# Fourier input and gate of each 256-token tile by seven block products instead of eight, with the gate transposed on TensorE and kept in DRAM

## The chip, the cores and the metric

The kernel runs on one core of one Trainium2 chip. The metric is the device time of one execution in microseconds (us). The engines are called PE (TensorE; PEld is its weight load), DVE (VectorE), ACT (ScalarE), POOL (GpSimd) and SP (SyncE, which issues most DMAs).

## The reference

One layer of a hybrid token mixer on 2048 latent tokens of width 1024, with 256 context tokens as a prefix. All in float32:

```python
h = modulate(rms_norm(x, g_pre[layer]), shift, scale)
f_in, f_gate, q, k, v, r_gate = jnp.split(h @ w_in[layer], IN_SPLITS, axis=-1)
...
u = f_in.reshape(bsz, length, N_FOURIER_GROUPS, FOURIER_GROUP)
mixed = jnp.real(jnp.fft.fft2(u, axes=(1, 3), norm='ortho'))
y = jnp.einsum('blgc,gcd->blgd', mixed, w_fourier)
return y * jax.nn.silu(f_gate)
...
y = jnp.concatenate([fourier, retention], axis=-1) @ w_out[layer]
x_next = x + gate * rms_norm(y, g_post[layer])
```

w_in has 3072 columns: six blocks of 512, in the order f, gate, q, k, v, r_gate. The change concerns `h @ w_in` for the first two, f and its gate, which are 2048 x 1024 by 1024 x 1024.

## The kernel before, in words

TensorE multiplies in a 32-bit form of lower precision, so every float32 operand is split into a high part (a copy on ACT) and a low part (the difference, on DVE or POOL), and every product is three matmuls: high by high, high by low, low by high. A projection (`proj`, L176 to L181) of 128 tokens by 512 columns is thus 8 blocks of the inner dimension by 3, 24 matmuls of 128x512.

The stages in the order of time. First the adaLN vectors and the context. Then a loop over tiles t = 1 to 7 of 256 tokens: the normed and modulated tile h is kept in DRAM, and k, v and r_gate of its two chunks are projected, with the tails of the retention states (`kv_tail1`, `kv_tail2`) between them. Then the f stage, a loop over eight tiles again, each made of the two chunks of 128 tokens that the first step of the Fourier transform pairs (`FB`): `hf_split` splits h as read back, `fin` projects f (pf, 2 times 24 matmuls of 128x512), `butterfly` makes the steps of the transform over tokens on DVE in the blocks R, and `fgate` makes the gate (pfg) with the weights as the stationary operand, 4 times 24 matmuls of 128x256. That leaves the gate transposed, channels on partitions, as the later stage needs it; ACT writes Silu of it into four tiles sg in SBUF. `gate_acc` and `gate_fin` (the adaLN gate of the output, two matmuls pg) are spread over the same loop.

Then follows a block whose order is written by hand for all engines (L1251 on). Four residue classes of the transform come one after the other, in the order 2, 1, 5, 0, each in four groups g: `ops_pair` makes its operands from R (two scaled copies ta and tb on ACT, sums on DVE, then for each of four sums bt a cast on ACT and a low part op, on DVE for the first and on POOL for the second of a pair); T (`cls_T`, pT) multiplies them by a table; Th and Tl are T's high and low part, made by ACT and DVE; Y (`cls_y`, pp and pq) multiplies by the folded Fourier weights (weo); POOL multiplies the result into sg (`gate`, L945). Generators in the list bg hold work for DVE, ACT and POOL, and `pull(n)` lets n steps of it run between two T's. In the block before, T and Y of the first two classes run beside the splits of the q weights (wq); then q of the last pair of chunks (`q_steps(7)`, four products of 24 matmuls of 128x256, each two followed by the rotation on DVE and POOL); then class 5 beside the first retention chunk; then class 0, the other chunks and the output projection.

PE's order in the f stage is left to the scheduler before and is written by hand after; DVE, ACT, POOL and SP are left to it there in both.

Of the kernel before, what the change touches and what calls it, by code (L numbers as in the profile page):

```python
# [10 lines left out]
F32 = mybir.dt.float32  # L11
# [19 lines left out]
def hymba_kernel(ctx: ExitStack, tc: tile.TileContext, a: dict, out: bass.AP):  # L31
# [12 lines left out]
    def unit(shape, dt, name):  # L44
        return units.tile(shape, dt, tag="unit", name=name)
# [7 lines left out]
    def lo_of(dst, src, hi):  # L53
        nc.vector.tensor_tensor(out=dst, in0=src, in1=hi.bitcast(F32), op=ALU.subtract)  # L54
# [471 lines left out]
    hraw = {}  # L526

    def h_load(t):
        hraw[t] = []
        for b in range(2):  # L530
            hr = w4.tile([P, KT, P], F32, tag="w4", name=f"hr{t}")
            nc.sync.dma_start(out=hr, in_=d_h[FB[t][b] // 2][:, :, FB[t][b] % 2 * P:(FB[t][b] % 2 + 1) * P])
            hraw[t].append(hr)

    def hf_split(t):
        hi, lo = unit([P, KT, 256], F32R, f"fhi{t}"), unit([P, KT, 256], F32R, f"flo{t}")
        for b, hr in enumerate(hraw.pop(t)):
            bs = slice(b * P, (b + 1) * P)
            nc.scalar.copy(hi[:, :, bs], hr)
            lo_of(lo[:, :, bs], hr, hi[:, :, bs])  # L540
        hls[t] = (hi, lo)
# [185 lines left out]
    for t in range(1, NT):  # L727
        hi, lo = hls.pop(t)
        for b in range(2):
            c = 2 * t + b  # L730
            tok = slice(b * P, (b + 1) * P)
            p1 = ps("pk")
            proj(p1, hi, lo, tok, wk_u)
            kr = kr_of(p1, c)
            kv_tail1(*pend[0])
            p2 = ps("pv")
            proj(p2, hi, lo, tok, wv_u)
            v = v_of(p2, c)
            kv_tail2(*pend[0])
            pend[:] = [(c, kr, v, *kv_operands(kr, v))]  # L740
            if b == 0 and t + 1 < NT:
                x_prep(t + 1)
            if b == 1 and t + 2 < NT:
                x_tile(t + 2)
            if t == 3 and b == 0:
                decay_tables()
            if t == NT - 1 and b == 0:
                wf_u, bg = load_w("wf", a["w_in"], 0)
                h_load(0)
            if t == NT - 1 and b == 1:  # L750
                hf_split(0)
                h_load(1)
            for f in bg[:3]:
                f()
            bg = bg[3:]
            p3 = ps("pr")
            proj(p3, hi, lo, tok, wr_u)
            rg_of(p3, c)


    wg_u, bg = load_w("wg", a["w_in"], 512)
    sg = [unit([P, SEQ], F32, f"sg{g}") for g in range(4)]
    R = [unit([P, 4, 512], F32, f"R{i}") for i in range(4)]

    def blk(j):
        return R[j // 4][:, j % 4, :]

    def fgate_g(t, g):
        hi, lo = hls[t]
        pg = ps("pfg", (P, 256))  # L770
        for kt in range(KT):
            whi = wg_u[kt // 2][:, 0, kt % 2, g * P:(g + 1) * P]
            wlo = wg_u[kt // 2][:, 1, kt % 2, g * P:(g + 1) * P]
            mm(pg, whi, hi[:, kt, :], start=(kt == 0), stop=False)  # L774
            mm(pg, whi, lo[:, kt, :], start=False, stop=False)  # L775
            mm(pg, wlo, hi[:, kt, :], start=False, stop=(kt == KT - 1))  # L776
        dst = sg[g].rearrange("p (b c n) -> p b c n", b=2, n=P)[:, :, FB[t][0], :]
        nc.scalar.activation(dst, pg.rearrange("p (b n) -> p b n", b=2), AF.Silu)
        if g == 3:
            hls.pop(t)  # L780

    def fgate(t):
        for g in range(4):
            fgate_g(t, g)

# [24 lines left out]

    def two(dst, x, y, sign):

        nc.vector.scalar_tensor_tensor(out=dst, in0=x, scalar=2.0, in1=y, op0=ALU.mult,
                                       op1=ALU.add if sign > 0 else ALU.subtract)
# [5 lines left out]
    def fin(t, b):  # L820
        hi, lo = hls[t]
        pf = ps("pf")
        proj(pf, hi, lo, slice(b * P, (b + 1) * P), wf_u)
        j = FB[t][0]
        if b == 0:
            nc.scalar.copy(blk(j), pf)
        else:
            tt(blk(j + 8), blk(j), pf, ALU.subtract)
            tt(blk(j), blk(j), pf, ALU.add)
# [136 lines left out]

    wfs = load_wf()
    h_load(2)
    for t in range(NT):
        if t + 1 < NT:  # L970
            hf_split(t + 1)
        if 0 < t and t + 2 < NT:
            h_load(t + 2)
        fin(t, 0)
        if t == 0:
            kv_tail1(*pend[0])
            for f in bg[:3]:
                f()
        fin(t, 1)
        if t == 0:  # L980
            kv_tail2(*pend[0])
            for f in bg[3:]:
                f()
        butterfly(t)
        if t < NT - 2:
            fgate(t)
        if 1 <= t <= 4:
            gate_acc(2 * (t - 1))
            gate_acc(2 * (t - 1) + 1)
        if t == 5:  # L990
            gate_fin()


# [39 lines left out]
    def q_steps(p):  # L1033
# [7 lines left out]
        def q(s):  # L1041
            if s % 2 == 0:
                pq.append(ps("pq"))
            o = pq[s // 2][:, s % 2 * 256:s % 2 * 256 + 256]
            for kt in range(KT):
                h = hq[p, kt // 4]
                whi = wq_u[kt // 2][:, 0, kt % 2, s * P:(s + 1) * P]
                wlo = wq_u[kt // 2][:, 1, kt % 2, s * P:(s + 1) * P]
                mm(o, whi, h[:, 0, kt % 4], start=(kt == 0), stop=False)  # L1049
                mm(o, wlo, h[:, 0, kt % 4], start=False, stop=False)  # L1050
                mm(o, whi, h[:, 1, kt % 4], start=False, stop=(kt == KT - 1))  # L1051
            if s % 2:
                rot_q(s // 2)
# [196 lines left out]

    with tc.manual_schedule(engines={ENG.PE, ENG.DVE, ENG.Activation, ENG.Pool, ENG.SP}):  # L1251
        load_tab(0)
        raw_q = w_load(a["w_in"], 1024)
        fgate_g(NT - 2, 0)
        bg.append(gen1(ops_pair(2)))
        pull(9)
        fgate_g(NT - 2, 1)
        fold_wf(*wfs)
        for g in range(2, 4):
            fgate_g(NT - 2, g)  # L1260
        load_tab(1)
        bg.append(gen1(ops_pair(1)))
        pull(2)
        fgate_g(NT - 1, 0)
        pull(2)
        fgate_g(NT - 1, 1)
        pull(2)
        fgate_g(NT - 1, 2)
        fgate_g(NT - 1, 3)
        pull(9)  # L1270
        wq_u = w_units("wq")
        load_h(7, 0)
        load_h(7, 1)
# [6 lines left out]
        for kt in range(KT):  # L1280
            bg.append(gen(lambda kt=kt: w_split(wq_u, kt, raw_q[kt // 2][:, kt % 2, :],
                                                eng=gp_ if kt % 2 and kt < 7 else nc.vector)))
            if kt == 3:
                bg.append(gen(lambda: split_h(7, 0)))
        bg.append(gen(lambda: split_h(7, 1)))
        pend = []
        for k in range(2):
            for g in range(4):
# [3 lines left out]
                pull(1)  # L1292
# [8 lines left out]
        for f in q_steps(7):  # L1301
            f()
# [234 lines left out]
```

## Time and profile before

| quantity | value |
|---|---|
| median of 3 runs | 925.33 us (925.31 to 925.96) |
| the profiled execution | 924.87 us |
| its span, first to last instruction | 923.0 us |
| PE matmuls, share of the span | 97%, 5412 of them |
| DVE / ACT / POOL, share of the span | 56% / 35% / 30% |
| mean granted clock of TensorE | 0.990 |

A row of the timeline gives the start, the duration, the engine and line, the output and inputs by the program's names, and in brackets how long the engine had been idle and what ended that. The duration of one matmul is longer than the distance of two starts, as matmuls are pipelined. The page cuts the span in 40 slices with the busy share of each in tenths. A row of windows gives the busy time of each engine in a stretch, with the number of instructions, and at its end the granted clock, the share of the DMA engines and GB/s. A row of groups ends with busy time, mean ns and the idle time just ahead.

### The profile page before, as it was taken

To read this page: it belongs to the slowest core of one execution; us is meant where nothing else is said; L and a number is where in the kernel's file an instruction comes from. 1 tells how busy PE (TensorE), PEld (TensorE's weight loads), DVE (VectorE), ACT (ScalarE), POOL (GpSimd) and SP (SyncE) were. 2 spreads that over 40 slices of the span, in tenths; PEclk is the share of its full clock that TensorE was granted. 3 is DMA by queue.
4 is the path that set the end of the run, shared out by engine and by line. 5 is a ranking of instruction groups with operands and counts; after the bars stand their busy time and mean duration, and the time that the engine had idled before them with its cause. 6 is when DMAs were issued, how large, how long until landed. Compare 5 with 4: busy or idle time off the path is not lost.

```text
span 923.0 us, 14211 instructions
## 1 busy us (share of the span) xinstructions
PE 898.6 (97%) x5412; PEld 788.5 (85%) x5412; DVE 517.8 (56%) x1020; ACT 325.6 (35%) x654; POOL 275.2 (30%) x342
## 2 busy tenths in 40 slices
PE   7899999999999999999999998999999999999997
PEld 6678888888888888999998898998888989989885
DVE  3455655254353842332512569998677767777552
ACT  3444862262222432211111153543243334333331
POOL 2106331222122111000000056765343434443352
PEclk8999999999999999999999999899999999999999
DMA  8935683363442843633311146579545554344412
GB/s 298 395 132 222 210 312 120 122 241 121 164 168 88 291 130 130 205 95 96 96 61 47 47 138 211 189 246 343 193 144 184 184 180 172 106 145 129 145 58 92
DMA packets 76309, 153.47 MB, mean 166 GB/s; under 512 B 6096, under 2 KB 32976, under 8 KB 70480
## 3 DMA queue, kind: packets, MB, share of 16 engines
q1 hardware_dynamic: 74976, 146.26, 45.9%
q0 software_dynamic: 1120, 6.29, 2.0%
q8 instruction: 43, 0.70, 0.3%
q14 instruction: 26, 0.21, 0.1%
q10 hardware_dynamic: 144, 0.00, 0.0%
HBM read 107.71 MB, written 44.83 MB: 165 GB/s over the span
## 4 chain that ended last, share of the span: by engine, by line
PE 84%; DVE 6%; DMA 4%; ACT 2%; issue 2%; POOL 1%; SPq 0%; DVEq 0%; POOLq 0%; ACTq 0%
PE pout L180 5%; PE pout L181 5%; PE pout L179 5%; PE pfg L776 3%; PE pfg L775 3%; PE pfg L774 3%; PE pr L179 3%; PE pr L180 3%; PE pf L179 3%; PE pf L180 3%; PE pr L181 3%; PE pf L181 3%; PE pv L179 3%; PE pv L181 3%; PE pk L181 3%; PE pv L180 3%
## 5 line engine op out<-in xcount | busy, mean ns | idle before, releaser
L179 PE MATMUL pout<-wo,y 128*128 128x512 f32 x256 | 102.0, 399 | 0.0
L180 PE MATMUL pout<-wo,y 128*128 128x512 f32 x256 | 99.8, 390 | 1.7 <-DVE wo L151 1.7
L181 PE MATMUL pout<-wo,y 128*128 128x512 f32 x256 | 100.1, 391 | 0.4 <-DVE y L54 0.4
L1051 PE MATMUL pq<-hq,wq 128*128 128x256 f32 x256 | 72.5, 283 | 0.6 <-DVE hq L54 0.6
L1049 PE MATMUL pq<-hq,wq 128*128 128x256 f32 x256 | 73.0, 285 | 0.0
L774 PE MATMUL pfg<-fhi,wg 128*128 128x256 f32 x256 | 72.7, 284 | 0.0
L1050 PE MATMUL pq<-hq,wq 128*128 128x256 f32 x256 | 72.5, 283 | 0.0
L775 PE MATMUL pfg<-flo,wg 128*128 128x256 f32 x256 | 72.3, 283 | 0.0
L776 PE MATMUL pfg<-fhi,wg 128*128 128x256 f32 x256 | 72.0, 283 | 0.0
L205 POOL TENSOR_TENSOR ka<-ka,kb 128x512 f32<-128x512 f32 x16 | 20.9, 1309 | 129.0 <-DVE kb L57 98.4
L241 POOL TENSOR_TENSOR vd<-v,dk 128x256 f32<-128x256 f32 x64 | 43.8, 715 | 51.8 <-ACT v L563 30.1
L226 DVE SCALAR_TENSOR_TENSOR Sf<-Sf,dk,pkv 128x128 f32<-128x128 f32 x64 | 19.3, 345 | 69.9 <-PE pkv L256 68.3
L180 PEld LDWEIGHTS pout<-wo,y 128*128 128x128 f32 x256 | 48.2, 188 | 11.4 <-DVE wo L151 2.1
L181 PEld LDWEIGHTS pout<-wo,y 128*128 128x128 f32 x256 | 48.0, 188 | 11.2 <-DVE y L54 0.9
L179 PEld LDWEIGHTS pout<-wo,y 128*128 128x128 f32 x256 | 48.2, 188 | 9.0
L1206 POOL TENSOR_TENSOR xo<-xo,t 128x512 f32<-128x512 f32 x30 | 44.4, 1500 | 22.8 <-DMA xo<-in_x 12.6
L179 PE MATMUL pf<-wf,fhi 128*128 128x512 f32 x128 | 50.4, 393 | 0.0
L856 POOL DMA_DIRECT2D tab<-in_tabs x4 | 2.6, 648 | 159.4 <-PE pf L181 159.4
L180 PE MATMUL pf<-wf,fhi 128*128 128x512 f32 x128 | 49.9, 389 | 0.0
L181 PE MATMUL pf<-wf,flo 128*128 128x512 f32 x128 | 49.8, 389 | 0.0
L1051 PEld LDWEIGHTS pq<-hq,wq 128*128 128x128 f32 x256 | 49.1, 192 | 0.8 <-DVE hq L54 0.8
L774 PEld LDWEIGHTS pfg<-fhi,wg 128*128 128x128 f32 x256 | 49.1, 192 | 0.5 <-issue 0.2
(293 smaller groups left out, 2550.4 us busy)
## 6 DMA issues: line engine op xcount, KB each, us to landing
sd<-d_st SPq DMA_DIRECT2D x16, 1024.0 KB, 5.5
wraw<-in_w_in SPq DMA_DIRECT2D x20, 512.0 KB, 5.1
ada<-in_ada_ss SPq DMA_DIRECT2D x8, 1024.0 KB, 12.9
hr<-d_h SPq DMA_DIRECT2D x16, 512.0 KB, 5.0
out<-xo SPq DMA_DIRECT2D x32, 256.0 KB, 2.1
xo<-in_x SPq DMA_DIRECT2D x30, 256.0 KB, 3.5
xtx<-in_xT SPq DMA_DIRECT2D x7, 1024.0 KB, 7.0
xk<-in_x SPq DMA_DIRECT2D x14, 512.0 KB, 6.1
```

The source lines that it names most:

```text
L179: mm(o, hi[:, kt, tok], whi, start=first, stop=False)
L180: mm(o, hi[:, kt, tok], wlo, start=False, stop=False)
L181: mm(o, lo[:, kt, tok], whi, start=False, stop=last)
L205: nc.gpsimd.tensor_tensor(out=ra, in0=ra, in1=rb.rearrange("p h a f -> p h (a f)"), op=ALU.add)
L241: nc.gpsimd.tensor_tensor(out=t[:, :, i, :], in0=v[:, hs, :], in1=d[:, hs].unsqueeze(2).to_broadcast([P, 2, P]), op=ALU.mult)
L774: mm(pg, whi, hi[:, kt, :], start=(kt == 0), stop=False)
L775: mm(pg, whi, lo[:, kt, :], start=False, stop=False)
L776: mm(pg, wlo, hi[:, kt, :], start=False, stop=(kt == KT - 1))
L1049: mm(o, whi, h[:, 0, kt % 4], start=(kt == 0), stop=False)
L1050: mm(o, wlo, h[:, 0, kt % 4], start=False, stop=False)
L1051: mm(o, whi, h[:, 1, kt % 4], start=False, stop=(kt == KT - 1))
L1206: nc.gpsimd.tensor_tensor(out=xo, in0=xo, in1=ch.t[j], op=ALU.add)
```

## The change

For one tile, h is a 2 x 2 matrix of blocks: two chunks of 128 tokens by two halves of the inner dimension (A11 to A22). The weights are 2 x 2 blocks of 512 x 512: two halves of the inner dimension by f and gate (B11 to B22). The four result blocks (f and gate of the two chunks) took eight block products; after the change they take seven, by Strassen's scheme in Winograd's form. The sums of weight blocks, T1 to T4, are made once by DVE beside tile 7 of the x loop, where they and B11, B21, B22 are split; the sums of h, S1 to S4, are made for each tile by `h_comb`, which runs for tile t + 1 while tile t is multiplied. A block product (`product`) is 12 matmuls of 128x512. The products of a tile accumulate in three PSUM banks, X, Y and Z; between two products into one bank its sum so far is copied by ACT (p1, u2, p5) or added up by DVE (fg, R).

The gate of a chunk now comes out with tokens on partitions. `fg_T` turns it by four TensorE transposes into PSUM during the next tile, ACT writes Silu of it to a work tile, and SP stores it to DRAM (d_sg); ahead of the T and Y stage it is loaded back as four tiles sg of 1 MB. `gate_acc` and `gate_fin` move into the x loop. The wq weights are split during the last tile, and q of pair 7 moves ahead of T(0,0), its rotation split in two steps (rots); `ops_pair(1)` comes after it, and two steps of the list are pulled after each T of the first class. The diff, cut to its core:

```diff
-    def fgate_g(t, g):
-        hi, lo = hls[t]
-        pg = ps("pfg", (P, 256))
-        for kt in range(KT):
-            whi = wg_u[kt // 2][:, 0, kt % 2, g * P:(g + 1) * P]
-            wlo = wg_u[kt // 2][:, 1, kt % 2, g * P:(g + 1) * P]
-            mm(pg, whi, hi[:, kt, :], start=(kt == 0), stop=False)
-            mm(pg, whi, lo[:, kt, :], start=False, stop=False)
-            mm(pg, wlo, hi[:, kt, :], start=False, stop=(kt == KT - 1))
...
+    def h_comb(t):
+
+        a11, a12, a21, a22 = hraw.pop(t)
...
+        hl_split(A["A11"], a11)
+        hl_split(A["A12"], a12)
+        tt(s1, a21, a22, ALU.add)
+        tt(s2, s1, a11, ALU.subtract)
+        hl_split(A["S2"], s2)
+        hl_split(A["S1"], s1)
+        hl_split(A["A22"], a22)
+        tt(a21, a11, a21, ALU.subtract)
+        hl_split(A["S3"], a21)
+        tt(a12, a12, s2, ALU.subtract)
+        hl_split(A["S4"], a12)
...
+    def b_T1():
+        for i in range(2):
+            x, y = b_load(0, 1, i), b_load(0, 0, i)
+            tt(x, x, y, ALU.subtract)
+            b_split("T1", i, x)
...
+    def b_T4():
+        for i in range(2):
+            x = b_load(1, 0, i)
+            less(x, "T2", i)
+            b_split("T4", i, x)
...
+    b_plain("B22", 1, 1)
+    h_comb(0)
+    h_raw(1)
+    b_T4()
+    rg_part(NCH - 1, hi, lo, toks[1])
...
+    def product(o, A, B, first):
+
+        for kt in range(4):
+            whi, wlo = B[kt // 2][:, 0, kt % 2, :], B[kt // 2][:, 1, kt % 2, :]
+            for i, (x, w) in enumerate(((0, whi), (0, wlo), (1, whi))):
+                mm(o, A[:, x, kt, :], w, start=(first and kt + i == 0),
+                   stop=(kt + i == 5), skip_group_check=not first)
...
+    def fg_T(t, b):
+
+        x, c = fgs.pop((t, b)), FB[t][b]
+        pt = ps("pfT")
+        for g in range(4):
+            nc.tensor.transpose(pt[:, g * P:(g + 1) * P], x[:, g * P:(g + 1) * P], ident)
+        s_ = wk([P, 4, P], "sgt")
+        nc.scalar.activation(s_, pt.rearrange("p (g n) -> p g n", g=4), AF.Silu)
+        nc.sync.dma_start(out=d_sg[:, :, c * P:(c + 1) * P].rearrange("g p n -> p g n"), in_=s_)
...
+        X = ps("pX")
+        product(X, A["A11"], Bw["B11"], True)
+        p1 = copy_of(X, "p1")
+        if t:
+            fg_T(t - 1, 1)
...
+        Y = ps("pY")
+        product(Y, A["A12"], Bw["B21"], True)
+        tt(blk(j), Y, p1, ALU.add)
+        if t:
+            fg_T(t - 1, 0)
...
+        product(X, A["S2"], Bw["T2"], False)
+        u2 = copy_of(X, "u2")
+        Z = ps("pZ")
...
+        h_comb(t + 1)
+        product(Z, A["S1"], Bw["T1"], True)
+        p5 = copy_of(Z, "p5")
+        product(X, A["S3"], Bw["T3"], False)
+        fg_sum(t, 1, X, p5)
+        product(Z, A["S4"], Bw["B22"], False)
+        fg_sum(t, 0, Z, u2)
+        product(X, A["A22"], Bw["T4"], False)
+        f_second(j, X)
+        butterfly(t)
+        if t + 2 < NT:
+            h_raw(t + 2)
...
-    for t in range(NT):
-        if t + 1 < NT:
-            hf_split(t + 1)
-        if 0 < t and t + 2 < NT:
-            h_load(t + 2)
-        fin(t, 0)
...
-        fin(t, 1)
...
-        butterfly(t)
-        if t < NT - 2:
-            fgate(t)
...
     with tc.manual_schedule(engines={ENG.PE, ENG.DVE, ENG.Activation, ENG.Pool, ENG.SP}):
...
+        X, Z, A = last["X"], last["Z"], last["A"]
+        product(Z, A["S1"], Bw["T1"], True)
+        p5 = copy_of(Z, "p5")
+        product(Z, A["S4"], Bw["B22"], False)
+        fg_sum(NT - 1, 1, X, p5)
+        fg_sum(NT - 1, 0, Z, last["u2"])
         bg.append(gen1(ops_pair(2)))
         pull(9)
-        fgate_g(NT - 2, 1)
+        rots = []
+        q7 = q_steps(7, rots)
+        q7[0]()
+        q7[1]()
+        fg_T(NT - 1, 1)
+        fg_T(NT - 1, 0)
+        sg = [unit([P, SEQ], F32, f"sg{g}") for g in range(4)]
+        for g in range(4):
+            nc.sync.dma_start(out=sg[g], in_=d_sg[g])
+        q7[2]()
         fold_wf(*wfs)
...
+        q7[3]()
+        rots[0]()
         load_tab(1)
         bg.append(gen1(ops_pair(1)))
...
-            bg.append(gen(lambda kt=kt: w_split(wq_u, kt, raw_q[kt // 2][:, kt % 2, :],
-                                                eng=gp_ if kt % 2 and kt < 7 else nc.vector)))
...
                 if len(pend) > 2:
                     Y(*pend.pop(0))
-                pull(1)
+                pull(2 - k)
+                if (k, g) == (0, 0):
+                    rots[1]()
                 if (k, g) == (0, 3):
                     bg.append(gen1(ops_pair(5)))
                     load_tab(2)
...
-        for f in q_steps(7):
-            f()
         bg.append(gen1(ops_even()))
```

How PE's instructions stand at the end of the f stage. Before, the last rows ahead of T(0,0) are the gate of tile 7 (pfg), and T's rows (pT) follow at once:

```order
L774 MATMUL pfg<-fhi_4396,wg_3269 128x256
L775 MATMUL pfg<-flo_4397,wg_3269 128x256
L776 MATMUL pfg<-fhi_4396,wg_3269 128x256
L917 MATMUL pT<-tab_4521,op_4557 128x2x128
L918 MATMUL pT<-tab_4521,op_4557 128x2x128
L919 MATMUL pT<-tab_4521,op_4557 128x2x128
```

After, these are the last two products of tile 7 (pX is the product with T3, pZ the ones with T1 and B22) and the first matmuls of q (pq):

```order
L892 MATMUL pZ<-T_3016,S_4390 128x512 x4
L892 MATMUL pX<-T_3133,S_4391 128x512 x6
L892 MATMUL pX<-T_3134,S_4391 128x512 x6
L892 MATMUL pZ<-T_3016,S_4390 128x512 x2
L892 MATMUL pZ<-B_3310,S_4391 128x512 x6
L892 MATMUL pZ<-B_3311,S_4391 128x512 x6
L1164 MATMUL pq<-hq_4562,wq_4542 128x256
L1165 MATMUL pq<-hq_4562,wq_4542 128x256
L1166 MATMUL pq<-hq_4562,wq_4542 128x256
```

Only two matmuls of the product with T1 are left between the product with T3 and the one with B22, which reuses Z; and q, which came after the Y's of the second class, now stands ahead of the T's.

How DVE's instructions stand from the first low part of T (Tl) on. Before, the operands of class 1 (op, from bt) are done by then, and the wq splits stand between the Tl and the y:

```order
L57 TENSOR_TENSOR bt<-R_3277,tb 128x512
L57 TENSOR_TENSOR bt<-R_3276,ta 128x512
L851 TENSOR_TENSOR op_4671<-bt,op_4671 128x512
L57 TENSOR_TENSOR bt<-R_3277,tb 128x512
L54 TENSOR_TENSOR Tl<-pT,Th 128x512
L149 TENSOR_TENSOR wq_4798<-wraw,wq_4798 128x512
L54 TENSOR_TENSOR Tl<-pT,Th 128x512 x2
L57 TENSOR_TENSOR y_4871<-p_sb,pq 128x256 x2
L149 TENSOR_TENSOR wq_4799<-wraw,wq_4799 128x512
L54 TENSOR_TENSOR Tl<-pT,Th 128x512
L57 TENSOR_TENSOR y_4905<-p_sb,pq 128x256 x2
```

After, the operands of class 1 and the second rotation of q (qa, qb, qt) stand there:

```order
L54 TENSOR_TENSOR Tl<-pT,Th 128x512
L901 SCALAR_TENSOR_TENSOR ta<-R_3395,ta 128x512
L901 SCALAR_TENSOR_TENSOR tb<-R_3396,tb 128x512
L57 TENSOR_TENSOR qa<-pq,qcs 128x512
L57 TENSOR_TENSOR qb<-pq,qcs 128x512
L1183 TENSOR_TENSOR qt<-qb,qa 64x256
L1183 TENSOR_TENSOR qt<-qa,qb 64x256
L54 TENSOR_TENSOR Tl<-pT,Th 128x512
L57 TENSOR_TENSOR bt<-R_3395,ta 128x512
L993 TENSOR_TENSOR op_4830<-bt,op_4830 128x512
L57 TENSOR_TENSOR bt<-R_3396,tb 128x512
L54 TENSOR_TENSOR Tl<-pT,Th 128x512
```

What moved is `ops_pair(1)`, from ahead of T(0,0) to between the T's, and the rotation, which came after the Y's; the wq splits went the other way.

How DVE's instructions stand in tile 0 of the f stage, which is new. The rows ahead of the sum fg that frees bank X (the last split of tile 0's own sums stands further up):

```order
L57 TENSOR_TENSOR braw<-braw,T_3130 128x1024
...
L57 TENSOR_TENSOR braw<-braw,T_3130 128x1024
L54 TENSOR_TENSOR A_3480<-hr_3345,A_3480 128x512
L57 TENSOR_TENSOR hs_3478<-hs_3477,hr_3343 128x512
L57 TENSOR_TENSOR hr_3347<-hr_3343,hr_3347 128x512
L54 TENSOR_TENSOR T_3355<-braw,T_3355 128x1024
L57 TENSOR_TENSOR R_3393<-pY,p_3414 128x512
L54 TENSOR_TENSOR T_3356<-braw,T_3356 128x1024
L57 TENSOR_TENSOR hr_3345<-hr_3345,hs_3478 128x512
L57 TENSOR_TENSOR fg<-pX,p_3514 128x512
```

braw are raw weight blocks on the way to T4 (T_3355, T_3356), and hr, hs and A_3479 belong to tile 1: all of this stands ahead of fg.

251 lines of the change are left out of this document (148 added, 103 removed).

## The prediction

> **What bounds the kernel now.** I read the page's first part, the slices, the chain and the groups; then the timeline of TensorE; then the windows of the stages that change. The page says that the matmul stream is nearly the span, and that the chain runs through it.
>
> ```profile
> PE 898.6 (97%) x5412; PEld 788.5 (85%) x5412; DVE 517.8 (56%) x1020; ACT 325.6 (35%) x654; POOL 275.2 (30%) x342
> PE   7899999999999999999999998999999999999997
> DVE  3455655254353842332512569998677767777552
> PE 84%; DVE 6%; DMA 4%; ACT 2%; issue 2%; POOL 1%; SPq 0%; DVEq 0%; POOLq 0%; ACTq 0%
> ```
>
> A slice is 23 us. In slices 16 to 22, counted from 0 (369 to 531 us, f and gate products), TensorE reads 9 and DVE 1 to 5 tenths: a matmul less there is time less. In slices 24 to 26 (554 to 623) DVE reads 9: the next stage is not TensorE's. The windows show it (columns: time, then busy time and count of PE, PEld, DVE, ACT and POOL, then the clock, DMA share and GB/s):
>
> ```profile
> 357.87:518.00 160.13, 160.13 (x984) 144.01 (x983) 50.73 (x65) 31.20 (x56) 0.81 (x1) 1.00 0.32 96
> 542.50:561.20 18.70, 17.70 (x146) 17.29 (x145) 14.20 (x24) 11.58 (x27) 14.58 (x16) 1.00 0.51 169
> 561.20:572.85 11.65, 11.65 (x99) 11.65 (x98) 10.96 (x12) 2.50 (x5) 7.94 (x9) 1.00 0.65 229
> 572.85:578.00 5.15, 2.72 (x15) 1.90 (x14) 4.40 (x7) 1.32 (x3) 3.04 (x3) 0.85 0.92 304
> 578.00:583.00 5.00, 5.00 (x25) 5.00 (x25) 4.87 (x8) 3.24 (x6) 3.98 (x5) 0.50 0.13 50
> 640.00:923.00 283.00, 275.61 (x1668) 245.54 (x1666) 184.92 (x443) 92.20 (x214) 112.39 (x124) 1.00 0.43 149
> ```
>
> The rows are f and gates; the T and Y of two classes; q of pair 7, 11.65 us of pure matmuls under which the operands of class 5 are made (DVE 10.96); the head of T(2,0), which waits; a stretch at half clock; and the rest. After 640 the TensorE is full again, so a lead gained earlier is kept to the end.
>
> **Term 1: matmuls.** Durations of single matmuls overlap, so I take the pitch of starts, and the counts from the groups (three rows a product; the first and last are shown).
>
> ```profile
> 339.82 0.39 PE L180 MATMUL pk<-wk,hhix 128*128 128x512 f32 x1
> ...
> 344.81 0.39 PE L181 MATMUL pk<-wk,hlox 128*128 128x512 f32 x1
> 345.05 0.60 PE L506 MATMUL pkT<-ident,ka 128*128 128x128 f32 x4
> ...
> 345.71 0.40 PE L180 MATMUL pv<-wv,hhix 128*128 128x512 f32 x1
> ...
> 419.80 0.28 PE L774 MATMUL pfg<-fhi,wg 128*128 128x256 f32 x1
> ...
> 426.88 0.28 PE L776 MATMUL pfg<-fhi,wg 128*128 128x256 f32 x1
> ```
>
> The groups of the page (count, then busy time and mean):
>
> ```profile
> L774 PE MATMUL pfg<-fhi,wg 128*128 128x256 f32 x256 | 72.7, 284 | 0.0
> L776 PE MATMUL pfg<-fhi,wg 128*128 128x256 f32 x256 | 72.0, 283 | 0.0
> L179 PE MATMUL pf<-wf,fhi 128*128 128x512 f32 x128 | 50.4, 393 | 0.0
> L181 PE MATMUL pf<-wf,flo 128*128 128x512 f32 x128 | 49.8, 389 | 0.0
> ```
>
> Wide: (344.81 − 339.82)/22 = 0.2268 us. Half wide: (426.88 − 419.80)/59 = 0.120. Removed: 384 × 0.2268 + 768 × 0.120 = 87.1 + 92.2 = 179.3. Added: 8 tiles × 7 products × 12 = 672 wide ones, 152.4, not 7/8 of 179.3, since a wide matmul is cheaper per column. Four transposes and the step behind them take 345.71 − 345.05 = 0.66, less one matmul 0.44; the gate needs 16 such groups, 7.1. Net 179.3 − 159.5 = **−19.8 us**. The Trainium skill, "TensorE: Matmul & The Clock Gate", Part 4, gives about 275 ns for a transpose in a kernel's context; by that 64 would take 17.6 us, as an estimate, and the term would be −9.3; the trace has 0.11 us each in a row of four and decides. The q of pair 7 and the two adaLN matmuls only move: zero, as both lie on TensorE before and after.
>
> **Term 2: new waits inside f.** A product reuses the bank that a copy or a sum must have read, and DVE now makes the operands of the next tile. The prices:
>
> ```profile
> 495.93 1.22 DVE L54 TENSOR_TENSOR flo<-hr,fhi 128x1024 fp32r<-128x1024 f32 x1
> 519.35 1.29 DVE L57 TENSOR_TENSOR R<-R,R 128x512 f32<-128x512 f32 x2
> ...
> 501.20 0.39 PE L181 MATMUL pf<-wf,flo 128*128 128x512 f32 x1
> 501.63 0.59 ACT L826 COPY R<-pf 128x512 f32<-128x512 f32 x1 [5.01 <-PE pf L181]
> ```
>
> A tile is 84 × 0.2268 + 2 × 0.44 = 19.9 us of TensorE. DVE has 7 lo parts, 4 combinations, 5 sums and about 3 butterfly passes, 19 of 128x512 at 0.61 to 0.68: 11.6 to 13; ACT 12 passes of 0.59, 7.1. Both fit, so middle tiles cost nothing, unless the order on DVE makes a sum late (rival 2). Two places have no room. Tile 0: the last product into X (A22·T4) waits for the sum fg, and that stands behind both halves of T4 and tile 1's first combinations: 4 subtractions at 1.15, 2 lo parts at 1.22 and 8 small passes at 0.605, 11.9 us from where the tile's own splits end. That is, by my walk, 8.3 us into the tile; fg is done at 20.2, the product could start at 18.3 (6 products, transposes and kv products at 0.12): +1.9, between 0 (splits end by 6.4) and 4. Last tile: between Z's end and the next product into Z only two matmuls stand, and the copy p5 needs 0.43 + 0.59 after the last start: 1.02, less the pitch, about +0.9, between 0.6 and 1.5. Sum **+2.8**. The splits of the B blocks (14 lo parts and 12 subtractions, 30 us at 1.15) lie beside tile 7's projections, where DVE is at 2 to 4 tenths (slices 14 and 15): zero, up to 2 if they run late into tile 0.
>
> **Term 3: the cover that q gave.** With q of pair 7 ahead, nothing of TensorE's is left between the Y's and T(2,0); the operands of classes 1 and 5 are made between the T's. Before, T(0,0) starts at 542.50 and T(2,0)'s head ends near 578.1, 35.6 us, of which q is 11.65: net 23.95. Its waits today:
>
> ```profile
> 574.36 0.38 PE L919 MATMUL pT<-tab,op 128*128 128x256 f32 x1 [0.75 <-POOL op L851]
> ...
> 577.55 0.58 PE L919 MATMUL pT<-tab,op 128*128 128x256 f32 x1 [0.82 <-POOL op L851]
> ```
>
> The same timeline for DVE and POOL, where one DVE pass coincides with a run of gates:
>
> ```profile
> 565.71 4.01 DVE L817 SCALAR_TENSOR_TENSOR tb<-R,tb 128x512 f32<-128x512 f32 x1
> ...
> 565.79 3.37 POOL L945 TENSOR_TENSOR sg<-y,sg 128x256 f32<-128x256 f32 x4
> ```
>
> And the groups by shape:
>
> ```profile
> L849 ACT CAST op<-bt 128x512 fp32r<-128x512 f32 x12 | 7.4, 620 | 23.2 <-DVE bt L57 23.2
> L851 POOL TENSOR_TENSOR op<-bt,op 128x512 fp32r<-128x512 f32 x6 | 7.7, 1288 | 29.1 <-ACT op L849 23.3 <-PE pq L1051 3.9 <-issue 1.9
> L57 DVE TENSOR_TENSOR y<-p_sb,pq 128x256 f32<-128x256 f32 x24 | 8.8, 407 | 0.0
> L1065 DVE TENSOR_TENSOR qt<-qa,qb 64x256 f32<-64x256 f32 x16 | 14.3, 891 | 0.4
> L1065 DVE TENSOR_TENSOR qt<-qb,qa 64x256 f32<-64x256 f32 x16 | 10.3, 646 | 0.7
> ```
>
> The DVE order after, from T(0,0) to the last operand of class 1: 13 wide passes at 0.605 (7.9), two qt (1.5) and two y (0.8), 10.2; one of them beside a run of gates takes 4.01 instead of 0.68 (+3.3): 13.5. DVE was busy 14.20 of 18.70 us in this stretch before, 76%, as it waits for each Th; 13.5/0.76 = 17.8. T(1,0) can't end before. From there to class 5's last operand on DVE: 12 passes (7.3) and ten y (4.1), 11.4, by the same share 15.0, and 19.3 with another lock; I take half a lock, 17.2. Then the ACT cast 0.62, the POOL lo 1.29 and T's last matmuls, 2.7. Sum 37.7, so 37.7 − 23.95 = **+13.8 us**. Bounds: busy without a gap or lock, 10.2 + 11.4 + 2.7 plus 4.5 of waits as before, 28.8 (+4.9); both locks, 39.8 (+15.9). I take 37.7, since the rows before show both the lock and the gaps. SP now queues 4 stores of gates and 4 loads of 1 MB behind the last Silu, while the second table lies behind POOL's qt's; they land under the same stretch and I add nothing, up to 2.
>
> **Sum.** −19.8 + 2.8 + 13.8 = −3.2. The profiled execution is 924.87 (span 923.0 and 1.87 around it), 0.46 under the median 925.33. So 925.33 − 3.2 = **922.1 us**.
>
> **Rivals.** *1. The cover wasn't needed.* DVE catches up because nobody waits for the y's and gates; the stage is at its floor, 28.8. Sum −19.8 + 2.8 + 4.9 = −12.1: 913.2. For: DVE has 56% of the span. Against: 9 tenths in this very stretch, and 4.01 us for one locked pass. Chance 0.22.
>
> *2. f is slowed (slower).* Seven products a tile hand their bank over through ACT and DVE; if in each of tiles 1 to 7 one product waits 1.2 us more for p1, u2, p5 or fg, because an in-order DVE puts a combination ahead of it, that is +8.4: 930.5. It decides from 3.2/7 = 0.46 us a tile on. Against: two banks' worth of other products stands between most of them. Chance 0.18.
>
> *3. The clock falls in f (slower).* In the rows above waits of 2.43 us within 5.15 are followed by 5 us at clock 0.50, which costs 2.5; waits of 1.0 in 18.7 left it at 1.00. If each of 7 tiles collects such waits, +17.5: 939.6. The Trainium skill, the same page, "A second HAM failure mode: psum-queue depth-cycling", tells that short idles of PE between groups that cycle PSUM banks make the clock oscillate and that the cost is paid between bursts; this speaks against the change's three banks. The trace's f stage shows no idle and can't test it. Chance 0.06.
>
> *4. The products don't fall to seven.* The order shows 84 wide matmuls a tile; chance 0.
>
> **Numbers.** Forecast 0.50 (918 to 926), rival 1 0.22, rival 2 0.18, rival 3 0.06, the rest 0.04. About 0.2% (1.85 us) is what a measurement here can tell from no change. Faster by that: 0.37 of the forecast, 0.22, 0.01 of the rest: 0.60. Within: 0.12 of the forecast, 0.06 of rival 2, 0.02: 0.20. Slower: 0.01, 0.12, 0.06 and 0.01: 0.20. The range takes in rival 1's point and, of rival 2, what lies under 0.9 us a tile: 913.0 to 928.5, with 0.5 + 0.22 + 0.06 + 0.02 inside.
>
> **What would show it.** Right: f from its first product to the last Z near 163 us (152.4, 14 transpose groups 6.2, the kv products 1.9, waits 2.8); T(0,0) at 542.50 − 19.8 + 2.8 + 11.65 = 537.2; idle time on T's matmuls up by about 12 us, released by POOL or ACT op and DVE Tl; a clock under 1 only there. Wrong: idle on pX or pZ in every tile (rival 2), PEclk under 1 in slices 16 to 22 (rival 3), or a head of T(2,0) that ends before 568, where I expect 574.9 (rival 1).

## The result and the profile after

The changed kernel takes 937.02 us (median of 4 runs, 936.42 to 938.68) against 925.32 us before (4 runs, 925.01 to 925.96). The ratio is 1.0128, with a 95% interval of 1.0111 to 1.0146: 11.7 us slower, where 922.1 was forecast. The profiled execution has a span of 935.1 us, 12.1 more than before. One of all the runs below, the fourth of `gates_out`, was in a slow state (1110.4 us at a mean granted clock of 0.744) and is left out of its median.

The page of the changed kernel, first part and slices (busy tenths; PEclk is the granted clock):

```profile
PE 890.2 (95%) x4996; PEld 762.5 (82%) x4996; DVE 590.3 (63%) x1126; ACT 353.3 (38%) x693; POOL 285.2 (30%) x343
PE   7899999999969999899999986898999999999997
DVE  3456675264352788855755587797767878676652
PEclk8899999999989999999999997799999999999999
```

416 matmuls are gone, as the change says, and DVE has 72 us more work. TensorE now has holes in two places that were full or nearly so: slice 11, counted from 0 (257 to 281 us), in the x loop, far ahead of the products that changed, and slices 23 to 25 (538 to 608 us), the T and Y stage; the clock is lower in slices 11, 24 and 25. The waits of TensorE name them (who waited for whom; sum, times, longest):

```profile
PE pg L813 <- DVE ones L806: 7.3, 1, 7.3
PE pT L1059 <- ACT op L991: 4.5, 4, 1.8
PE pT L1059 <- DMA tab<-in_tabs: 3.1, 1, 3.1
PE pp L1080 <- DVE Tl L54: 3.1, 2, 2.7
PE pX L892 <- DVE fg L57: 3.0, 1, 3.0
PE pT L1061 <- POOL op L993: 2.1, 3, 0.9
PE pZ L892 <- ACT p L906: 0.7, 1, 0.7
```

The largest has nothing to do with Strassen's scheme. pg is the adaLN gate, which the change moved into the x loop. The timeline of TensorE there:

```profile
261.17 0.38 PE L111 MATMUL pr<-ident,rstd 128*128 128x128 f32 x2
268.85 3.75 PE L813 MATMUL pg<-GG,ones 128*128 128x512 f32 x4 [7.30 <-DVE ones L806]
271.62 1.42 PE L179 MATMUL pr<-wr,hhix 128*128 128x512 f32 x1
```

And of DVE, in the same microseconds:

```profile
261.89 2.28 DVE L116 TENSOR_TENSOR xtx<-xtx,pr 128x2048 f32<-128x2048 f32 x1
...
265.62 2.35 DVE L124 TENSOR_SCALAR xtx<-xtx,m 128x256 f32<-128x256 f32 x7
267.88 0.68 DVE L54 TENSOR_TENSOR vlo<-vd,vhi 128x512 fp32r<-128x512 f32 x1
268.54 0.17 DVE L806 MEMSET ones<- 128x128 f32 x1
```

`gate_fin` fills a tile with ones, 0.17 us of work. DVE reaches it only behind the modulation of the next tile, and on TensorE the r_gate products of chunk 10 stand behind pg. So all of TensorE waits 7.3 us for a constant, and then runs at half clock for a while (granted clock 0.50 from 268.85 to 272.60): 3.75 us for four matmuls that took 1.88 before, when they stood in the f loop:

```profile
494.26 1.88 PE L807 MATMUL pg<-GG,ones 128*128 128x512 f32 x4
```

The f stage begins at 369.9 instead of 357.9.

The stages from there (windows as before):

```profile
369.87:536.88 167.01, 163.31 (x745) 134.29 (x744) 102.77 (x157) 59.37 (x107) 8.95 (x7) 0.99 0.38 114
536.88:550.61 13.73, 13.73 (x106) 12.76 (x105) 10.94 (x17) 4.99 (x10) 2.56 (x2) 1.00 0.01 4
550.61:592.00 41.39, 27.45 (x165) 24.38 (x164) 31.95 (x50) 14.80 (x32) 26.11 (x27) 0.74 0.70 258
640.00:935.00 295.00, 286.48 (x1734) 254.80 (x1732) 198.69 (x471) 99.56 (x230) 118.91 (x132) 1.00 0.46 156
```

The first row is the products of f and gate: 163.3 us busy out of 167.0. The third is T and Y of the first two classes up to the head of class 5: 27.5 us of matmul in 41.4, at a mean granted clock of 0.74. What bounds the two comparable pieces can be read off two rows of each kernel: the first T of class 0 (its operands are called ope) and the first product of f. Before, and then after:

```profile
L917 PE MATMUL pT<-tab,ope x16: 278/283/363, 586.9 to 603.6; 128*128 128x256 f32 x16
L179 PE MATMUL pf<-wf,fhi x128: 389/389/798, 357.9 to 517.1; 128*128 128x512 f32 x128
```

The changed kernel:

```profile
L1059 PE MATMUL pT<-tab,ope x16: 278/283/363, 599.2 to 615.9; 128*128 128x256 f32 x16
L892 PE MATMUL pX<-B,A x96: 389/389/628, 369.9 to 518.4; 128*128 128x512 f32 x96
```

From the first product of f to class 0: 586.9 − 357.9 = 229.0 us before and 599.2 − 369.9 = 229.3 after. From class 0 to the end: 336.1 and 335.9. So 20 us of TensorE's work, and with the two moved pg matmuls 1.9 us more, were taken out of this stretch and it did not become shorter at all, and 12 us were added ahead of it. The experiments ask about both.

### The profile page after: what moved, and what is told of

It reads as the page before. It is cut to its first block, busy times and chain, and to the rows that moved or that the text cites. A ratio compares the mean times of both kernels' runs of the same rounds, so it can differ in the third digit from the quotient of the medians.

```text
span 935.1 us, 13679 instructions
## 1 busy us (share of the span) xinstructions
PE 890.2 (95%) x4996; PEld 762.5 (82%) x4996; DVE 590.3 (63%) x1126; ACT 353.3 (38%) x693; POOL 285.2 (30%) x343
## 5 line engine op out<-in xcount | busy, mean ns | idle before, releaser
L892 PE MATMUL pX<-T,S 128*128 128x512 f32 x276 | 68.5, 398 | 3.0 <-DVE fg L57 3.0
L241 POOL TENSOR_TENSOR vd<-v,dk 128x256 f32<-128x256 f32 x64 | 48.5, 787 | 52.4 <-ACT v L628 31.8
L892 PEld LDWEIGHTS pX<-T,S 128*128 128x128 f32 x276 | 51.9, 191 | 14.0 <-DVE fg L57 3.5
L149 POOL TENSOR_TENSOR wq<-wqr,wq 128x512 fp32r<-128x512 f32 x4 | 6.7, 1700 | 149.6 <-ACT wq L143 149.5
L1166 PEld LDWEIGHTS pq<-hq,wq 128*128 128x128 f32 x256 | 49.0, 192 | 1.0 <-DVE hq L54 1.0
L1165 PEld LDWEIGHTS pq<-hq,wq 128*128 128x128 f32 x256 | 49.1, 192 | 0.5 <-issue 0.2
L1164 PEld LDWEIGHTS pq<-hq,wq 128*128 128x128 f32 x256 | 49.1, 192 | 0.5 <-issue 0.2
L1296 ACT ACTIVATE t<-pout 128x512 f32<-128x512 f32 x32 | 19.0, 595 | 74.2 <-PE pout L181 58.5
L179 PE MATMUL pr<-wr,hhix 128*128 128x512 f32 x112 | 45.4, 405 | 0.0
L179 PE MATMUL pv<-wv,hhix 128*128 128x512 f32 x112 | 44.8, 400 | 0.0
```

The source lines that it names most:

```text
L179: mm(o, hi[:, kt, tok], whi, start=first, stop=False)
L241: nc.gpsimd.tensor_tensor(out=t[:, :, i, :], in0=v[:, hs, :], in1=d[:, hs].unsqueeze(2).to_broadcast([P, 2, P]), op=ALU.mult)
L892: mm(o, A[:, x, kt, :], w, start=(first and kt + i == 0), stop=(kt + i == 5), skip_group_check=not first)
L1296: nc.scalar.activation(ch.t[j], ch.po[j], AF.Square, scale=1.0 / 32.0, accum_out=ch.ss[:, j:j + 1])
```

## The experiments

All twelve are given with their medians against the kernel before, which on the chips of these runs had medians of 925.35 to 925.85. The times below move more from run to run than those of the first comparison (the runs of one kernel span 1.3 to 5.9 us), so the length from the first product of f to class 0 is given beside them from each one's own profile: it leaves out what varies at the start of the program. The last two columns divide it at the end of f's last product (the last pf before, the last product into X after). The runs stem from three chips; each ratio compares two kernels on one chip, and a difference of two medians below can be off by 1 to 2 us where the chips differ.

| kernel | us, median | ratio to before, 95% interval | f to class 0, us | f's first to last product, us | from there to class 0, us |
|---|---|---|---|---|---|
| before | 925.32 | 1 | 229.0 | 160.0 | 69.0 |
| changed | 937.02 | 1.0111 to 1.0146 | 229.3 | 163.0 | 66.3 |
| gate_only | 935.56 | 1.0094 to 1.0124 | 226.2 | 158.3 | 67.9 |
| ones_early | 928.42 | 1.0023 to 1.0053 | 231.3 | 163.2 | 68.1 |
| gate_back | 927.08 | 1.0006 to 1.0029 | 229.3 | 161.2 | 68.1 |
| t4_first | 925.44 | 0.9992 to 1.0019 | 227.9 | 160.6 | 67.3 |
| tab_early | 926.90 | 0.9991 to 1.0018 | 228.4 | 160.6 | 67.8 |
| z_late | 923.04 | 0.9954 to 0.9980 | 226.2 | 159.7 | 66.5 |
| lean | 925.35 | 0.9977 to 1.0002 | 228.2 | 164.8 | 63.4 |
| gates_out | 921.92 | 0.9934 to 0.9968 | 225.0 | 160.6 | 64.4 |
| q_back | 923.11 | 0.9966 to 0.9988 | 224.3 | 158.5 | 65.8 |
| warm | 923.43 | 0.9973 to 1.0000 | 225.0 | 158.0 | 67.0 |
| fold_mid | 919.99 | 0.9924 to 0.9960 | 222.3 | 158.3 | 64.0 |
| both | 922.57 | 0.9956 to 0.9980 | 224.3 | 157.6 | 66.7 |

**The gate's place.** `gate_only` is the kernel before with `gate_acc` and `gate_fin` taken from the f loop into the x loop, with nothing of Strassen's:

```diff
+            if 1 <= t <= 4:
+                gate_acc(2 * (t - 1) + b)
+            if t == 5 and b == 0:
+                gate_fin()
             p3 = ps("pr")
             proj(p3, hi, lo, tok, wr_u)
...
-        if 1 <= t <= 4:
-            gate_acc(2 * (t - 1))
-            gate_acc(2 * (t - 1) + 1)
-        if t == 5:
-            gate_fin()
```

> The kernel before, with only the adaLN gate (the eight accumulations and the two products pg) moved into the x loop, to where the change has it. Theory W: the change loses about 10 us because pg stands in PE's order ahead of r_gate of chunk 10 and waits for a memset of ones that DVE reaches only behind the modulation of the next tile (7.3 us of wait), and then runs at half clock (about 2.7 more). Then this kernel shows the same wait and comes to 935 us. Rival V: the x loop was short of DVE time anyway, in this place of the changed kernel only because other new work stands there; the move by itself is free: 925 us, within 2.

It took 935.56, theory W's number, and its trace has the same wait to the hundredth:

```profile
269.57 2.90 PE L746 MATMUL pg<-GG,ones 128*128 128x512 f32 x3 [7.30 <-DVE ones L739]
```

It also has pg ahead of the f stage, as the changed kernel does: beside its 226.2 us from f to class 0 the changed kernel's 229.3 are not the same length but 3.1 us more.

`ones_early` is the changed kernel with the memset two half tiles of the x loop earlier (two, not the four that its expectation names), at t = 4 instead of t = 5:

```diff
     def gate_fin():
-        ones = wk([P, P], "ones")
-        nc.vector.memset(ones, 1.0)
+        ones = ones_g[0]
...
+        if kt == 6:
+            ones_g.append(cst.tile([P, P], F32, name="ones_g"))
+            nc.vector.memset(ones_g[0], 1.0)
```

> The changed kernel, with the tile of ones made four half tiles of the x loop earlier, in a buffer of its own. W: pg finds its operands, 937.0 - 10.1 = 927 us (925.5 to 928.5). V: the wait goes to the next matmul that needs the modulated tile, and the time stays at 935 to 937.

928.42: 8.6 us less, no wait at pg, f begins at 360.3. W holds; 1.5 us of the 10.1 are given back, in the profile behind T(0,0), which starts 9.4 us earlier while class 0 starts 7.6 earlier. `gate_back` undoes the move altogether:

```diff
-            if 1 <= t <= 4:
-                gate_acc(2 * (t - 1) + b)
-            if t == 5 and b == 0:
-                gate_fin()
...
             f_tile(t)
+            if 1 <= t <= 4:
+                gate_acc(2 * (t - 1))
+                gate_acc(2 * (t - 1) + 1)
+            if t == 5:
+                gate_fin()
```

> The changed kernel with the whole adaLN gate back in the f loop, behind tiles 1 to 5, as before. W: 927 us, as with the early ones, plus what pg waits for in the f loop, where DVE has 8 us to spare in a tile: 927 to 930. V: 935 to 937.

927.08, 1.4 us above the kernel before on the same chip (925.68): the move of a piece that I had priced at nothing is the whole of the loss but that. What is left of the change, the seven products with the new order behind them, is no faster than eight.

**Tile 0.** `t4_first` is `ones_early` with the weight sum T4 ahead of tile 0's splits:

```diff
+    b_T4()
     h_comb(0)
     h_raw(1)
-    b_T4()
```

> The changed kernel with the early ones and with the weight sum T4 made ahead of the splits of tile 0 instead of behind them. Theory W says that tile 0's wait of 3.0 us for the sum fg, and the 2.4 us that the half clock after it costs, come from the work on T4 standing ahead of fg on DVE: 927 - 5.4 = 921.6 us (920.5 to 923). Rival U: T4's 7 us of DVE are then in the way of tile 0's own splits, and the first product waits instead: 926 to 930.

925.44, 3.0 less than `ones_early` where 5.4 were expected. The wait for fg is gone, with its half clock, but another stands in its place, the one for the first copy p1. On ACT p1 stands behind casts of tile 0's own sums, which DVE makes only after T4's passes, from 365.29 on; ACT is idle for 2.65 us there, and p1 starts at 368.40:

```profile
PE pX L896 <- ACT p L910: 2.5, 1, 2.5
```

So U holds in part. This kernel shows most cleanly what the change is worth without the misplaced gate and the late T4: nothing (0.9992 to 1.0019). T(0,0) starts at 537.8 in its trace, where I had worked out 537.2. The gain is there at this point; it is lost behind it.

**The table.** `tab_early` loads the table of class 1 ahead of q instead of behind it:

```diff
         bg.append(gen1(ops_pair(2)))
+        load_tab(1)
         pull(9)
...
-        load_tab(1)
         bg.append(gen1(ops_pair(1)))
```

> The kernel with early ones and T4 first (925.4 us, T(0,0) at 537.8, T(1,0) waiting 4.0 us for its table, class 0's T at 587.0), and the second table now loaded ahead of q, so that it doesn't share the DMA engines with the 4 MB of gates that come back from DRAM. Theory C: from the last product into X to class 0 the time is set by one chain over DVE, ACT and POOL (operands of class 2, the rotation, operands of class 1, the T's and Y's, operands of class 5); the table only makes T(1,0) late, whose second operand is late anyway: a gain of 1 to 2 us, 923.4 to 924.4. Rival D: the late table is what holds the stage; 4 us less, 921.4.

926.90, no gain: neither D's 4 us nor the 1 to 2 us that I expected of C. The wait for the DMA (4.0 us in `t4_first`) disappears from the trace; the waits of T for ACT's op grow from 4.2 to 6.7 us and those for POOL's from 2.3 to 3.0. D falls: the table, though late, was late together with other things.

**Where the chain begins.** `z_late` starts from `t4_first` and puts the last product that f needs ahead of the one with T1:

```diff
             f_second(j, p4)
+            product(Z, A["S1"], Bw["T1"], True)
             butterfly(t)
             last.update(X=X, Z=Z, A=A, u2=u2)
             return
...
         X, Z, A = last["X"], last["Z"], last["A"]
-        product(Z, A["S1"], Bw["T1"], True)
```

> The kernel with early ones and T4 first, and in the last tile the product with T3, the last that f needs, ahead of the product with T1, 2.3 us earlier. Theory C: the chain starts 2.3 us earlier, but DVE meets the folded weights and q's rotation, which wait for TensorE's q products and for the two pw matmuls, and gives the 2.3 us back there: 925 us, within 1. Rival D2: the chain runs through and the end comes 2.3 us earlier, 923.1.

923.04, 2.4 less than `t4_first`, the 2.3 of D2; the intervals of the two ratios lie apart. TensorE does the same work; only when the last product of f ends has changed, and the end of the kernel moved with it. In its own profile f ends only 0.9 us earlier; in the four later kernels with this order f's products take 157.6 to 158.5 us, for 160.6 in the three without it. My reading that DVE would give the time back at the rotation fell.

**Two parts of the chain.** `lean` combines four edits:

```diff
-        wfs.extend(load_wf())
+        fold_wf(*load_wf())
...
+        load_tab(1)
         pull(9)
...
+            product(Z, A["S1"], Bw["T1"], True)
             butterfly(t)
...
         bg.append(gen1(ops_pair(1)))
+        pull(3)
```

> The kernel with early ones and T4 first, with four things together: the second table ahead of q, the product with T3 ahead of T1, the Fourier weights folded beside the last tile of f instead of behind q, and three steps of class 1's operands ahead of T(0,0). Theory C: DVE no longer waits for TensorE between the operands of class 2 and class 1, so the chain is 2.3 + 2.1 (its wait for the folded weights) + 1.3 (their two passes) shorter, and the table costs nothing: 925.4 - 5.7 - 1.5 = 918.2 us (916 to 921), faster than the kernel before. Rival P: TensorE's own work up to T(0,0) and the half clock set the time; 923 to 926.

925.35, far from the expected 918.2. The profile puts the loss ahead of f's end: the Fourier weights now had to come by DMA in time for pw in the middle of the last tile, ahead of the products of f, which take 164.8 us with it. From there to class 0 is the shortest of all, 63.4 us.

```profile
PE pw L1051 <- DMA wfa<-in_wf: 3.1, 1, 3.1
```

`gates_out` is `t4_first` with POOL's multiplications by the gate left out for classes 1 and 2:

```diff
         def gate(d, y):
-            nc.gpsimd.tensor_tensor(out=d, in0=y, in1=d, op=ALU.mult)
+            if r not in (1, 2):
+                nc.gpsimd.tensor_tensor(out=d, in0=y, in1=d, op=ALU.mult)
```

> The kernel with early ones and T4 first, with POOL's multiplications by the gate left out for classes 1, 2 and 5's half (all of the classes whose residue is 1 or 2). Theory C with the shared port: DVE passes that take 1.25 instead of 0.68 us beside the gates (eight in this stretch) go back to 0.68, and POOL's operand parts come at once: 8 x 0.57 = 4.6 us less, 920.8 (919 to 922.5). Rival: the gates run beside the waits for ACT and TensorE, and nothing comes of it: 924.5 to 926.

921.92 (921.4 to 922.7): 3.5 of the 4.6 us. In the changed kernel a DVE pass beside those gates takes 1.25 us,

```profile
573.35 1.25 DVE L901 SCALAR_TENSOR_TENSOR ta<-R,ta 128x512 f32<-128x512 f32 x1
```

while POOL runs

```profile
573.19 2.17 POOL L1087 TENSOR_TENSOR sg<-y,sg 128x256 f32<-128x256 f32 x2
```

and 0.68 us elsewhere. In `gates_out` all of these passes take 0.68:

```profile
560.22 0.68 DVE L905 SCALAR_TENSOR_TENSOR ta<-R,ta 128x512 f32<-128x512 f32 x1
```

So POOL's work is part of what holds this stage. Whether by the longer passes on DVE or by the gates ahead of POOL's own op was not taken apart.

**Is it q's place, or the clock?** `q_back` starts from `z_late` and puts q of pair 7 back behind the Y's:

```diff
-        q7 = q_steps(7, rots)
-        q7[0]()
-        q7[1]()
         fg_T(NT - 1, 1)
...
-        q7[2]()
         fold_wf(*wfs)
-        q7[3]()
-        rots[0]()
...
+        for f in q_steps(7):
+            f()
         bg.append(gen1(ops_even()))
```

> The kernel with early ones, T4 first and T3 ahead of T1 in the last tile (923.0 us), and q of pair 7 back behind the Y's of the second class, where it stood before the change. Theory C (a chain over DVE, ACT and POOL from the last product into X to class 5 sets the time, not TensorE): TensorE then stands idle for some 10 us ahead of T(0,0), which waits for class 2's operands, and has q as cover for class 5's; the chain is the same work in another order, and the time stays within 2 us: 921 to 925. Rival Q: putting q ahead is what lost the gain, since class 5's operands lost their cover; with q back the time falls by 5 us or more, to 918 or less. Rival R: TensorE's idle 10 us ahead of T(0,0) are lost for good: 930 or more.

923.11, to be compared with 923.04 (ratios 0.9977 and 0.9967): 11.65 us of matmuls moved across the T and Y stage, and the time is the same within 1 us. Q and R fall, C stands. TensorE did not even stand idle for 10 us as I had thought: T(0,0) started at 529.59, when class 2's operands came, and the slack lay between the T's.

```profile
529.59 0.38 PE L1064 MATMUL pT<-tab,op 128*128 128x256 f32 x1 [1.28 <-ACT op L996]
```

`warm` starts from `z_late` and adds 16 wide matmuls where TensorE waits:

```diff
+        def warm(n):
+            o = ps("warm")
+            for i in range(n):
+                mm(o, wq_u[0][:, 0, 0, 0:P], wq_u[i % 4][:, 0, 1, :], start=(i == 0),
+                   stop=(i == n - 1))
...
+                if (k, g) == (1, 0):
+                    warm(8)
...
+            if g == 0:
+                warm(8)
             pend.append((2, g, T(2, g)))
```

> The kernel with early ones, T4 first and T3 ahead of T1 (923.0 us), with eight matmuls more, on operands that lie there, ahead of T(1,0) and again ahead of T(2,0), whose result nobody reads. They run where TensorE waits. Theory H: the half clock after those waits (0.74 and 0.77 in these stretches) lengthens T's and Y's that the chain needs; the 16 matmuls keep the clock up, and the time falls by 2 to 4 us, 919 to 921. Theory C alone: the chain is on DVE, ACT and POOL, and the clock doesn't matter: 922 to 924. Rival: they delay the T's by their own 1.8 us each: 925 to 927.

The clock rose. `z_late` and then `warm`, the same two stretches:

```profile
536.00:560.00 24.00, 17.58 (x111) 15.13 (x110) 17.32 (x28) 8.88 (x18) 10.99 (x12) 0.83 0.73 285
560.00:587.00 27.00, 20.88 (x136) 19.39 (x136) 20.52 (x34) 11.49 (x25) 20.09 (x20) 0.77 0.48 160
```

With the added matmuls:

```profile
536.00:560.00 24.00, 18.51 (x118) 16.67 (x117) 18.49 (x30) 8.47 (x17) 12.81 (x15) 0.86 0.78 292
560.00:587.00 27.00, 21.55 (x150) 20.08 (x150) 20.51 (x36) 12.84 (x25) 19.00 (x19) 0.94 0.56 194
```

From 0.77 to 0.94 in the second, and the time is 923.43: neither the higher clock nor 3.6 us of matmuls more (16 × 0.2268) shows as a gain or a loss (by the ratios it is 0.9986 for 0.9967, with overlapping intervals). H falls. In this kernel's T and Y stage TensorE and its clock are not the limit.

**A shorter chain.** `fold_mid` starts from `z_late`, folds the Fourier weights between the last two products, and pulls three steps of class 1's operands ahead of T(0,0):

```diff
             product(Z, A["S1"], Bw["T1"], True)
+            fold_wf(*wfs)
             butterfly(t)
...
         q7[2]()
-        fold_wf(*wfs)
         q7[3]()
...
         bg.append(gen1(ops_pair(1)))
+        pull(3)
```

> The kernel with early ones, T4 first and T3 ahead of T1 (923.0 us), with the Fourier weights folded between the last products with T1 and B22 (their load has come by then, unlike in the run with four things together, where pw waited 3.1 us for it), and three steps of class 1's operands ahead of T(0,0). Theory C: 2 to 4 us less, 919 to 921. Rival: DVE's passes are only put in another order; 922 to 924.

919.99, 0.9924 to 0.9960 of the kernel before: 5.3 us faster, the best of all, and again without less work on TensorE. `both` adds the early table and two times ten matmuls:

```diff
+        load_tab(1)
         pull(9)
...
+                if (k, g) == (1, 0):
+                    warm(10)
```

> The run before with the second table ahead of q and ten matmuls that nobody reads ahead of T(1,0) and T(2,0). Theories C and H together: 916 to 919 us. C alone: 919 to 921, as without them.

922.57, 2.6 more than `fold_mid`, against both expectations. The profiles point at the added matmuls. In `fold_mid` T(1,0) starts without a wait, and here only behind the first ten of them:

```profile
552.29 0.41 PE L1065 MATMUL pT<-tab,op 128*128 128x256 f32 x1
...
555.29 0.27 PE L1065 MATMUL pT<-tab,op 128*128 128x256 f32 x1
```

From T(0,0) to class 0 it takes 47.3 us, for 44.6 in `fold_mid` and 44.8 in `lean`, which has the early table and no added matmuls. In `warm` TensorE still waited 2.1 us for the table behind the first eight, so these were free. A run with the table alone was not made.

## Why the prediction was wrong

*Term 1 held.* The middle tiles of f run without a wait. In the changed kernel's timeline of TensorE two successive transposes of the same kind lie 19.99 us apart; 19.9 was forecast.

```profile
398.69 0.60 PE L916 MATMUL pfT<-ident,fg 128*128 128x128 f32 x4
...
418.68 0.60 PE L916 MATMUL pfT<-ident,fg 128*128 128x128 f32 x4
```

The next product starts at 399.04, 0.35 us behind the first transpose of its group, and over the whole tile a group costs (19.99 − 84 × 0.2268)/2 = 0.47 us, 0.12 for a transpose, where 0.11 was forecast. The 275 ns of the Trainium skill ("TensorE: Matmul & The Clock Gate", Part 4) are near the duration of a single one here (272 ns on average), but not what a transpose in a row of four costs. Rivals 2 and 4 did not happen. Nor did rival 3: three PSUM banks in turn leave the clock at 1.00 from tile 1 on, so the Trainium skill's rule on cycling banks ("A second HAM failure mode: psum-queue depth-cycling", the same page) found no idle to act on in these tiles.

*The step that failed* is the last sentence of term 1: "The q of pair 7 and the two adaLN matmuls only move: zero, as both lie on TensorE before and after." For q it held (`q_back`). For the adaLN gate it cost 10.1 us: f began 12.0 late, of which 1.9 are the matmuls themselves. I counted the instructions on the engine that they run on, and not the queue of the engine that feeds them: the memset of ones is one more instruction of the moved step, and DVE's queue in the x loop was 7 us long at that point, where in the f loop pg waited for nothing. `gate_only` shows that this alone takes the kernel before to 935.6.

*Term 2* was 2.8 and the f stage was 3.7 longer than worked out, 167.0 for 163.3. The two waits were found and sized nearly right (3.03 for 1.9, 0.68 for 0.9). What was missing is the clock behind the first:

```profile
391.51 4.37 PE L892 MATMUL pX<-T,S 128*128 128x512 f32 x12 [3.03 <-DVE fg L57]
395.67 3.17 PE L892 MATMUL pX<-B,A 128*128 128x512 f32 x12
398.69 0.60 PE L916 MATMUL pfT<-ident,fg 128*128 128x128 f32 x4
```

24 matmuls take 398.69 − 391.51 = 7.18 us instead of 24 × 0.2268 = 5.44: 1.7 us for one wait of 3 us (granted clock 0.66 over the first twelve). About 1 us is left that I can't place.

*Term 3* had the right sign and most of the size, but not the mechanism. From T(0,0) to the copy behind the head of T(2,0), before and after:

```profile
578.17 0.59 ACT L927 CAST Th<-pT 128x512 fp32r<-128x512 f32 x1 [2.07 <-PE pT L919]
```

The changed kernel:

```profile
550.97 0.28 PE L1059 MATMUL pT<-tab,op 128*128 128x256 f32 x1
...
591.49 0.59 ACT L1069 CAST Th<-pT 128x512 fp32r<-128x512 f32 x1 [1.75 <-PE pT L1061]
```

That is 40.5 us, for 37.7 forecast and 39.8 as the upper bound. The cost over before is 40.5 − 24.0 = 16.5, not 13.8. The floor of 28.8, on which rival 1 stood, was far off. I had described the loss as cover that q gave. `q_back` says otherwise: q's place makes no difference. The stage from the last product of f to class 0 is a chain over DVE, ACT and POOL, and it starts when f of the last tile is done. Before, 24.6 us of gate products stood between f's end and T(0,0) and hid the first part of it. The change merges f and gate, so f's last product comes at the end of the merged work, and the chain starts no earlier than it did: 163.0 us behind f's first product, for 160.0 before. From there to class 0, before and after:

```profile
517.91:586.92 69.01, 65.58 (x506) 63.39 (x504) 58.12 (x85) 29.63 (x61) 36.41 (x36) 0.95 0.40 133
532.90:599.21 66.31, 51.70 (x335) 46.74 (x334) 52.20 (x84) 24.54 (x48) 31.86 (x31) 0.82 0.53 192
```

TensorE is busy there for 14 us less, although its clock is lower, and the stretch is only 2.7 us shorter. The gate products were taken from beside this chain.

*The sum.* −3.2 forecast for the time, plus 10.1 (gate), 3.7 (f) and 2.7 (T and Y), less 1.0 between T(2,0) and class 0 and 0.2 behind it, makes +12.1, the difference of the spans. The range ended at 928.5; without the moved memset (`ones_early`, 928.42) the time would have been at its upper end, and the forecast of a gain would still have been wrong, since the chain behind f gives nothing back. That a gain of TensorE's work is carried behind 640 us held: from class 0 to the end all these kernels take 335.3 to 337.2 us.

What stays open: whether the early table has a part in the 2.6 us of `both`; and how much of the chain could be taken out by moving operands of classes 1 and 5 still further, which was not tried.

## What to carry to other kernels

A step that only moves costs nothing on the engine it runs on, and can still cost its producers' queue: for every instruction that the step issues, a memset too, read what stands ahead of it on its own engine at the new place, and what stands behind its consumer. And before counting saved matmuls, find the last result that the next stage waits for: work taken from beside a serial chain is worth nothing, while ending that one result 2.3 us earlier was worth 2.4 us, and taking two passes and a wait off the chain, with three operand steps drawn forward, 2 to 3 us more. Merging two products into one scheme also merges their ends; the operand that others wait for should be finished first.

## What the runs showed of the hardware

One idle gap of 7.3 us on TensorE cost 2.8 us more, with a granted clock of 0.50 for the next 3.75 us, and one of 3.0 us cost 1.7 us, with 0.66 for the next 4.16 us. The 2.5 us wait in `t4_first` cost nothing behind it that shows (granted clock 1.00 from 369 to 390): its next twelve matmuls have 3.02 us in the timeline, as the twelve behind the 0.68 us wait do:

```profile
369.03 3.02 PE L896 MATMUL pX<-T,S 128*128 128x512 f32 x12 [2.47 <-ACT p L910]
...
520.84 3.02 PE L896 MATMUL pZ<-B,S 128*128 128x512 f32 x12 [0.68 <-ACT p L910]
```

A table of 1 MB, for which the kernel before took 5.5 us (the median of its four), took 9.9 us (issued at 555.10, its reader released at 564.97) while 4 MB of gates came back from DRAM; the start is in POOL's timeline,

```profile
555.10 0.57 POOL L998 DMA_DIRECT2D tab<-in_tabs  x1
```

and the end in TensorE's:

```profile
564.97 0.55 PE L1059 MATMUL pT<-tab,op 128*128 128x256 f32 x1 [3.14 <-DMA tab<-in_tabs]
```
